# A lora-up on 128 rows, its decay map on ScalarE, and chunk ends stored by ScalarE's queue

## The chip, the cores and the metric

The kernel runs on one core of a Trainium2 chip. A core has five engines with a queue of instructions each, which run side by side and wait for each other by semaphores: TensorE (PE: matrix products into the accumulator memory PSUM; its weight loads are listed apart as PEld), VectorE (DVE), ScalarE (ACT), GpSimd (POOL) and SyncE (SP), which here only issues memory transfers (DMAs). ScalarE and GpSimd can issue DMAs too. The metric is the device time of one execution in microseconds (us), the median over runs.

## What is computed

One layer of a diffusion backbone over 128 context and 2048 latent tokens of width 1024, in float32. The part that the change touches is the preparation of the operands of a bidirectional RWKV-7 scan, for two directions e, from low-rank ("lora") projections:

```python
lw = jnp.tanh(jnp.einsum('btd,edl->betl', hf, lp['decay_down']))
w = lp['decay_w0'][None, :, None, :] + jnp.einsum('betl,elc->betc', lw, lp['decay_up'])
decay = jnp.exp(-jnp.exp(-jax.nn.softplus(-w) - 0.5))
la = jnp.einsum('btd,edl->betl', hf, lp['iclr_down'])
a = jax.nn.sigmoid(lp['iclr_bias'][None, :, None, :] + jnp.einsum('betl,elc->betc', la, lp['iclr_up']))
kk = _heads(kf * lp['kk_scale'])
kk = kk * lax.rsqrt(jnp.maximum(jnp.sum(kk * kk, axis=-1, keepdims=True), 1e-24))
kd = kf[:, None] * (1.0 + (a - 1.0) * lp['ka_scale'])
```

`decay_up` and `iclr_up` are 64 x 512 for each direction. The log of the decay is -0.6065 sigmoid(w) (DEC is exp(-0.5)), and the kernel takes sigmoid(w) as (tanh(w/2) + 1) / 2. It sums it along time inside chunks of 64 tokens; exponentials of that sum scale the scan's operands.

## The kernel before

Three phases follow each other: `phase1` (projections, lora, short convolution; to about 920 us), `phase2` (the scan in 17 stages) and `phase3` (output projection). Phase 1 goes three times (`THIRD`) over two blocks of tokens, five blocks of 384 and the last of 256. In each pass group A (the scan's operands) runs over four groups g of 128 channels and the two blocks j; so there are 24 calls of `groupA`, "blocks" below. Group B (the convolution) follows.

All products are float32 split into a high part (float32r) and a rest. A dense product (lines 157 to 159) is 24 products of 128 x 128 weights on a block's columns. In `groupA` TensorE makes, by their accumulators' names: k (mmk), r (mmr), eight lora-up products (up), the head sum of k squared (pss, line 201 on the high part hsh and line 202 on the rest hsl), v (mmv), the gate g (mmg), a second head sum for the bonus (psb, the same two lines), and three transposes of v (psv, line 403).

`lup` makes a lora-up in two products. `lora_down` has laid x out on 128 partitions so that, for direction d, rows 64d to 64d + 63 hold the high part and the other 64 the rest. The first (line 355) multiplies by the weights' high part, which lies on both halves; the second (line 356) by the weights' rest, on the 64 rows with the high part of x alone. `load_up` splits the weights: the rests of both directions share one tile, one on each half.

Then, for each direction: tanh on ScalarE (361), the affine map on VectorE (362), the sum along time on VectorE (365 or 367), two exps on ScalarE (370 into pp, with a column for the shift; 371 in place), products on VectorE into four rotating buffers sp, each stored by SyncE's queue (`spill`). Line 382 stores the last column of each chunk of pp, 128 x 6 values, by SyncE's queue too. `part_sum` splits what it sums: the high part by ScalarE (193), the rest by GpSimd (194) into hsl, one buffer for all. `shifted` copies the accumulator into a padded row buffer (rawl, three of them) and sums neighbours on GpSimd (313: shk, shr, shv). Transposed v goes without its mean to vt (413, one buffer), stored by line 414. `gate_rows` makes the output gate beside group B.

The order on each engine is not that of the source. A scheduler in the build places every instruction by a model of time, so an edit moves instructions far from it as well; each engine then runs its queue strictly in that order.

Of the kernel before, what the change touches and what calls it, by code (L numbers as in the profile page):

```python
# [18 lines left out]
DEC = 0.6065306597126334  # L19
# [30 lines left out]
def phase1(K):  # L50
    nc, tc, A, S = K.nc, K.tc, K.A, K.S
    V, G, P, T = nc.vector, nc.gpsimd, nc.scalar, nc.tensor
    cp = Pool(K, "p1c", "left")
    wp = Pool(K, "p1w", "left", 2)
    hl = Pool(K, "p1h", "left", 2)
    tp = Pool(K, "p1t", "left")
    ca = Pool(K, "p1ca", "right")
    hr = Pool(K, "p1hr", "right")
    ta_ = Pool(K, "p1ta", "right")
# [5 lines left out]
    make_identity(nc, idt)  # L65
    vec = cp.tile([128, NV], F32, name="vec")
    nc.sync.dma_start(vec[:], A["vec"])
    ones = ta_.tile([128, 128], F32, tag="upraw", name="ones", bufs=1)
    nc.sync.dma_start(ones[:], A["cst"][:, 0:128])
    onr = cp.tile([128, 128], F32R, name="onr")  # L70
    V.tensor_copy(onr[:], ones[:])
# [4 lines left out]
    V.memset(eps[:], 1e-6)  # L76
    nln2 = cp.tile([128, 1], F32, name="nln2")
    V.memset(nln2[:], -0.6931471805599453)
    dv = cp.tile([128, ND], F32, name="dv")

    def ts(o, i, s1, s2=None, o0=ALU.mult, o1=ALU.add, eng=V):
# [20 lines left out]
    def load_up():  # L102

        raw = ta_.tile([128, 2, 2, 512], F32, tag="x", name="upraw", bufs=1)
        for h in range(2):
            nc.sync.dma_start(raw[h * 64:h * 64 + 64], A["wup"].rearrange("n (d p) c -> p n d c", d=2))
        parts = ca.tile([128, 6, 512], F32R, tag="upx", name="ups")
        hi, lo = parts[:, 0:4].rearrange("p (n d) c -> p n d c", d=2), parts[:, 4:6]
        for n in range(2):
            V.tensor_copy(hi[:, n], raw[:, n])  # L110
            for d in range(2):
                r = slice(d * 64, d * 64 + 64)
                V.tensor_tensor(lo[r, n], raw[r, n, d], hi[r, n, d].bitcast(F32), ALU.subtract)
                up[n, d] = (hi[:, n, d], lo[:, n])

    kept = set()

# [71 lines left out]
    def parts_of(t_, n, nm, eng):  # L189

        hi = ta_.tile([128, 384], F32R, tag="hsh", name=f"hsh{nm}", bufs=1)
        lo = ta_.tile([128, 384], F32R, tag="hsl", name=f"hsl{nm}", bufs=1)
        P.copy(hi[:, :n], t_[:, :n])  # L193
        eng.tensor_tensor(lo[:, :n], t_[:, :n], hi[:, :n].bitcast(F32), ALU.subtract)  # L194
        return hi, lo
# [25 lines left out]
    hsl = [hr.tile([128, 8, 512], F32, tag="h", name="wadas0")]  # L221
# [14 lines left out]
    for i, b in enumerate((0, 2, 1, 3)):  # L236
        pr = pmm.tile([128, 512], F32, tag="mm", name=f"psrow{b}")
        for k2 in range(2):
            wt = hsl[i][:, k2 * 4:k2 * 4 + 4] if i < 3 else hsl[k2 + 1][:, 8:12]
            nc.sync.dma_start(wt, A["wada"][b][:, k2 * 4:k2 * 4 + 4])  # L240
            mod_rows(pr, wt, range(k2 * 4, k2 * 4 + 4))
        if i == 0:
            x0 = load_x(0)
        if i == 1:
            wlora = [load_w(32), load_w(33)]
            x1 = load_x(1, ca, "upx")
        if i == 2:
            ws0 = [load_w(cb) for cb in (4, 0)]
        rows = ta_.tile([128, 512], F32, tag="upraw", name=f"modrow{b}", bufs=1)
        V.tensor_copy(rows[:], pr[:])  # L250
        hf = b % 2
        if hf not in psm:
            psm[hf] = pax.tile([128, 8, 2], F32, tag="ax", name=f"psmod{hf}")
        for cb in range(4):
            T.matmul(psm[hf][:, b // 2 * 4 + cb, :], rows[:, cb * 128:(cb + 1) * 128], sel[:], start=True, stop=True)
        if b >= 2:

            gs = cp.tile([128, 4, 2], F32, name=f"gs{hf}")
            sh = cp.tile([128, 4, 2], F32, name=f"sh{hf}")
            ad = lambda v: vec[:, v + hf * 4:v + hf * 4 + 4].unsqueeze(2).broadcast_to((128, 4, 2))  # L260
            V.tensor_tensor(sh[:], psm[hf][:, 0:4, :], ad(V_BSH), ALU.add)
# [12 lines left out]
    first_products(wlora + ws0, range(4, 8))  # L274


    NRAW = 3
    rawl = [cp.tile([128, 6, 66], F32, name=f"rawl{i}") for i in range(NRAW)]
    rawc = [cp.tile([128, 130], F32, name=f"rawc{i}") for i in range(1)]
    for t_ in rawl:  # L280
# [46 lines left out]
    def groupA(g, j, ws, hh, lw, pre):  # L327
        t0, n = BLK[j]
# [16 lines left out]
        rS = shifted(psr or dense(wr_, hh, n, "r"), j, 0, g, "r", 1)  # L345
        kds = []
        for d in range(2):
            rows = slice(d * 64, d * 64 + 64)
            cs = slice(g * 128, g * 128 + 128)

            def lup(which):
                ps = pmm.tile([128, 384], F32, tag="mm", name=f"up{which}_{K.u()}")
                hi, lo = up[which, d]
                x = lw[which * 2 + d]
                T.matmul(ps[:, :n], hi[:, cs], x[:, :n], start=True, stop=False)
                T.matmul(ps[:, :n], lo[rows, cs], x[rows, :n], start=False, stop=True)
                return ps

            psw = lup(0)
            t = tl("t", 2)  # L360
            P.activation(t[:, :n], psw[:, :n], AF.Tanh, bias=dcol(D_W0H + d * 4 + g), scale=0.5)
            V.tensor_scalar(t[:, :n], t[:, :n], -0.5 * DEC, -0.5 * DEC, ALU.mult, ALU.add)
            c = t
            if d == 0:
                V.tensor_tensor_scan(c[:, :n], smask[:, :n], t[:, :n], 0.0, ALU.mult, ALU.add)
            else:
                V.tensor_tensor_scan(c[:, :n][:, ::-1], smask[:, :n], t[:, :n][:, ::-1], 0.0, ALU.mult, ALU.add)
            pt = rot(pp[d], "pp")
            c3 = c[:, :n].rearrange("p (a b) -> p a b", b=64)
            P.activation(pt[:, :nch, 1 - d:65 - d], c3, AF.Exp)  # L370
            P.activation(c[:, :n], c[:, :n], AF.Exp, bias=nln2[:], scale=-1.0)
            psa = lup(1)
            ta = tl("ta", 2)
            P.activation(ta[:, :n], psa[:, :n], AF.Tanh, bias=dcol(D_IBH + d * 4 + g), scale=0.5)
            v3 = lambda x_: x_[:, :n].rearrange("p (a b) -> p a b", b=64)
            al = tl("sp", 4)
            V.tensor_tensor(v3(al), v3(kk), pt[:, :nch, d:64 + d], ALU.mult)
            spill(f"al{d}", g, j, al, "al")
            rh = tl("sp", 4)
            V.tensor_tensor(v3(rh), v3(rS), pt[:, :nch, 1 - d:65 - d], ALU.mult)  # L380
            spill(f"rh{d}", g, j, rh, "rh")
            nc.sync.dma_start(S[f"pc{d}"][g * 128:(g + 1) * 128, t0 // 64:t0 // 64 + nch], pt[:, :nch, 64 - 64 * d])
# [8 lines left out]
            V.scalar_tensor_tensor(be[:, :n], ta[:, :n], 1.0, kkn[:, :n], ALU.add, ALU.mult)  # L391
# [113 lines left out]
    def gate_rows():  # L505
        for b in range(2):
            pr = pmm.tile([128, 512], F32, tag="mm", name=f"psgr{b}")
            for k2 in range(4):
                wt = wp.tile([128, 2, 512], F32, tag="wr", name=f"wgate{b}{k2}", bufs=2)
                nc.sync.dma_start(wt[:], A["wada"][4 + b][:, k2 * 2:k2 * 2 + 2])  # L510
                mod_rows(pr, wt, (k2 * 2, k2 * 2 + 1))
                yield
            rows = ta_.tile([128, 512], F32, tag="upraw", name=f"gaterow{b}", bufs=1)
            P.copy(rows[:], pr[:])
            pg = pmm.tile([2, 512], F32, tag="mm", name=f"psgate{b}")
            T.matmul(pg[:], sel[:], rows[:], start=True, stop=True)
            gr = ta_.tile([2, 512], F32, tag="upraw", name=f"gate{b}", bufs=1)
            nc.sync.dma_start(gr[:], A["bgate"][:, b * 512:(b + 1) * 512].broadcast_to((2, 512)))
            V.tensor_tensor(gr[:], pg[:], gr[:], ALU.add)
            nc.sync.dma_start(S["gate"][:, b * 512:(b + 1) * 512], gr[:])  # L520


    up = {}
# [818 lines left out]
```

## Time and profile before

| | us |
|---|---|
| runs of before | 1814.86, 1816.56, 1825.39; median 1816.56 |
| the profiled execution | 1812.69 |
| its span, first to last instruction | 1810.9 |
| mean granted TensorE clock | 0.968 of full speed |
| group A, first, middle and last pass | 69 to 245, 407 to 602, 744 to 900 |

Engines' busy time counts neither waiting nor the issue of DMAs. TensorE's products overlap in the records: each lasts about twice the distance to the next start, so its speed is read from starts. A timeline row has start, duration, engine, source line, operation, tiles out<-in, rows*columns of the weights where it is a product, shapes, and in brackets the idle time before it and what ended it. DMA rows show the issue; the time from issue to landing stands apart.

### The profile page before, as it was taken

How to read it: one execution, taken by the hardware profiler on the slowest of the kernel's cores; microseconds unless marked ns; L12 is line 12 of the kernel's file. 1: busy time of each engine (PE TensorE's matmuls, PEld its weight loads, DVE VectorE, ACT ScalarE, POOL GpSimd, SP SyncE). 2: the span in 40 equal slices, each digit the busy share in tenths (PEclk: the TensorE clock that was granted, in tenths of full speed). 3: DMA queues.
4: the chain of work that ended last, by engine and by line, in shares of the span. 5: the costliest groups of instructions: out<-in, count | busy, mean ns of one | idle time of the engine just before them, and what ended most of it. 6: DMA issues, size and time to landing. Idle time of an engine off the chain costs nothing. (4 is left out here: it accounts for less than half of the span.)

```text
span 1810.9 us, 35097 instructions
## 1 busy us (share of the span) xinstructions
PE 1695.7 (94%) x13424; PEld 1534.4 (85%) x13424; DVE 1227.7 (68%) x2281; ACT 818.9 (45%) x1559; POOL 593.7 (33%) x1091
## 2 busy tenths in 40 slices
PE   5999999999999999999999899998998999898998
PEld 2988889999888999989999888888888888676886
DVE  5889987547877445588833457687777888858443
ACT  4555544214444122254431366666566666542222
POOL 0122210002222000122218247767676777322221
PEclk7899999999999999999999999999999999898999
DMA  9778886655666634487767466567668765645442
GB/s 355 215 231 236 236 244 241 234 212 143 186 180 185 187 121 144 135 234 233 202 229 263 107 146 160 145 178 164 156 167 177 178 159 131 169 154 186 144 147 93
DMA packets 315528, 335.36 MB, mean 185 GB/s; under 512 B 166936, under 2 KB 263704, under 8 KB 301280
## 3 DMA queue, kind: packets, MB, share of 16 engines
q1 hardware_dynamic: 278640, 324.20, 61.1%
q10 hardware_dynamic: 35360, 4.46, 1.6%
q0 software_dynamic: 1360, 4.46, 0.7%
q8 instruction: 106, 1.74, 0.4%
q14 instruction: 62, 0.51, 0.1%
HBM read 221.22 MB, written 111.82 MB: 184 GB/s over the span
## 5 line engine op out<-in xcount | busy, mean ns | idle before, releaser
L877 POOL TENSOR_TENSOR zt<-zt,ztmp 128x30 f32<-128x30 f32 (+7 forms) x510 | 205.6, 403 | 39.2
L949 PE MATMUL psE<-str,stl 128*128 128x128 f32 x1088 | 154.7, 288 | 12.5 <-DVE E L950 10.9
L949 PEld LDWEIGHTS psE<-str,stl 128*128 128x128 f32 x1088 | 136.0, 197 | 19.3 <-DVE E L950 12.1
L874 POOL TENSOR_TENSOR ztmp<-ab,zt 128x60 f32<-128x60 f32 (+7 forms) x255 | 135.3, 531 | 19.4
L722 ACT COPY bd<-rr 64x512 f32<-64x512 f32 x136 | 83.9, 617 | 79.4 <-PE psF L835 24.7
L950 DVE TENSOR_TENSOR E<-psE,msk 128x512 f32<-128x512 f32 x136 | 93.4, 689 | 26.4 <-PE psE L949 23.9
L313 POOL TENSOR_TENSOR shk<-rawl 128x384 f32<-128x384 f32 (+1 forms) x24 | 21.8, 908 | 251.7 <-ACT rawl L309 248.2
L996 PE MATMUL psS<-sv,E 128*64 128x64 f32 x1056 | 94.2, 237 | 8.2 <-DVE sv L1008 7.0
L962 PE MATMUL psY<-E,sv 128*64 128x64 f32 x1088 | 98.3, 233 | 2.2 <-DVE E L950 2.2
L996 PEld LDWEIGHTS psS<-sv,E 128*64 128x64 f32 x1056 | 68.4, 139 | 34.3 <-DVE sv L1008 11.2
L1008 DVE TENSOR_TENSOR sv<-psS,pc 64x128 f32<-64x128 f32 x254 | 72.4, 285 | 30.7 <-PE psS L996 22.7
L1278 POOL TENSOR_TENSOR z<-z,x 128x512 f32<-128x512 f32 x32 | 42.8, 1340 | 137.8 <-DVE z L1274 102.7
L835 PE MATMUL psG<-rr,bd 128*128 128x128 f32 x544 | 79.6, 287 | 7.2 <-DVE F L836 5.6
L835 PE MATMUL psF<-rr,bd 128*128 128x128 f32 x544 | 79.0, 287 | 7.1 <-issue 5.0
L938 PE MATMUL psX<-F,zb 128*128 128x128 f32 x544 | 73.3, 284 | 10.1 <-DVE E L950 5.8
L835 PEld LDWEIGHTS psG<-rr,bd 128*128 128x128 f32 x544 | 68.9, 195 | 10.6 <-DVE F L836 5.9
L938 PEld LDWEIGHTS psX<-F,zb 128*128 128x128 f32 x544 | 65.9, 195 | 13.8 <-DVE E L950 6.8
L962 PEld LDWEIGHTS psY<-E,sv 128*64 128x64 f32 x1088 | 71.9, 139 | 6.7 <-issue 3.7
L835 PEld LDWEIGHTS psF<-rr,bd 128*128 128x128 f32 x544 | 68.6, 196 | 10.2 <-issue 6.6
L157 PE MATMUL mmv<-h,w 128*128 128x384 f32 (+1 forms) x192 | 68.0, 354 | 4.4 <-ACT q1r L311 4.4
L194 POOL TENSOR_TENSOR hslb<-kd,hshb 128x384 fp32r<-128x384 f32 (+1 forms) x24 | 25.2, 1050 | 134.5 <-ACT hshb L193 133.0
L157 PE MATMUL mmg<-h,w 128*128 128x384 f32 (+1 forms) x192 | 63.6, 331 | 4.3 <-ACT rawc L316 2.3
(315 smaller groups left out, 5380.0 us busy)
## 6 DMA issues: line engine op xcount, KB each, us to landing
w<-scr_wsp SPq DMA_DIRECT2D x68, 1024.0 KB, 6.9
scr_wsp<-w SPq DMA_DIRECT2D x34, 1024.0 KB, 6.4
rr<-scr_ops SPq DMA_DIRECT2D x64, 512.0 KB, 4.8
scr_ops<-sp SPq DMA_DIRECT2D x160, 192.0 KB, 4.9
wr<-in_win SPq DMA_DIRECT2D x34, 512.0 KB, 6.9
ab<-scr_at SPq DMA_DIRECT2D x34, 256.0 KB, 4.1
x<-in_x SPq DMA_DIRECT2D x17, 512.0 KB, 4.0
wadas<-in_wada SPq DMA_DIRECT2D x8, 1024.0 KB, 13.1
```

The lines of the kernel that those rows point to most:

```text
L157: T.matmul(ps[:, :n], w[:, 0, k], hh[:, 0, k, :n], start=k == 0, stop=False)
L722: (V.tensor_copy if k in ON_DVE else P.copy)(dst, src)
L835: T.matmul(ps[:, i, :].rearrange("p (a b) -> p a b", b=64), w[:, u, :], x[:, :, u, :], start=True, stop=True)
L874: G.tensor_tensor(tv, ab[:, j:j + 2, j + 2:32].unsqueeze(1).broadcast_to((128, kn, 2, n)), zt[:, :kn, j:j + 2].unsqueeze(3).broadcast_to(( ...
L877: G.tensor_tensor(zt[:, :kn, j + 2:32], zt[:, :kn, j + 2:32], tv[:, :, r], ALU.subtract)
L938: T.matmul(px[:, i, :], B.zb[:, gi, us.start + i, :], g.F[:, us.start + i, :], start=True, stop=True)
L949: T.matmul(pe[:, i, hd, :].rearrange("p (b t) -> p b t", b=2), g.lt[:, :, hd, us.start + k + i].rearrange("p b t -> p (b t)"), g.rt[:, :, ...
L950: V.tensor_tensor(g.E[n][:, k:k + 2].rearrange("p a b c -> p (a b) c"), pe[:].rearrange("p a b c -> p (a b) c"), B.msk[:, ME[g.d]].unsquee ...
L962: T.matmul(ys[gi][hd * 64:(hd + 1) * 64, u, :], v[:, hd, :], e[:, hd, 64:128], start=True, stop=True)
L996: T.matmul(sp[r, hd, :], g.E[n][:, k, hd, 0:64], sv[:, u, hd, :], start=True, stop=True)
L1008: V.tensor_tensor(dst, sp[r], B.pc[r, 2 * p:2 * p + 2, c:c + 1].broadcast_to((64, 2, 64)), ALU.mult)
L1278: (V if last else G).tensor_tensor(z[:, cs], z[:, cs], xt[:, cs], ALU.add)
```

## The change

Four things are edited. `load_up` makes the weights' rest on 128 rows for both directions, and `lup` multiplies it with all of x. The affine map on VectorE becomes an activation that adds 1 on ScalarE, and its factor moves into the scales of the two exps. The chunk ends are stored by ScalarE's queue. And four kilobytes a partition are found for the longer tile: hsl shares vt's buffer, there are two padded row buffers instead of three, and rows of 512 (ones, modrow, gaterow, gate) share the buffer of group B's pv.

```diff
@@ phase1
-    ones = ta_.tile([128, 128], F32, tag="upraw", name="ones", bufs=1)
+    ones = tp.tile([128, 128], F32, tag="pv", name="ones", bufs=1)
...
+    one1 = cp.tile([128, 1], F32, name="one1")
+    V.memset(one1[:], 1.0)
@@ load_up
-        parts = ca.tile([128, 6, 512], F32R, tag="upx", name="ups")
-        hi, lo = parts[:, 0:4].rearrange("p (n d) c -> p n d c", d=2), parts[:, 4:6]
+        parts = ca.tile([128, 8, 512], F32R, tag="upx", name="ups")
+        hi, lo = [parts[:, i:i + 4].rearrange("p (n d) c -> p n d c", d=2) for i in (0, 4)]
         for n in range(2):
             V.tensor_copy(hi[:, n], raw[:, n])
+            V.tensor_tensor(lo[:, n], raw[:, n], hi[:, n].bitcast(F32), ALU.subtract)
             for d in range(2):
-                r = slice(d * 64, d * 64 + 64)
-                V.tensor_tensor(lo[r, n], raw[r, n, d], hi[r, n, d].bitcast(F32), ALU.subtract)
-                up[n, d] = (hi[:, n, d], lo[:, n])
+                up[n, d] = (hi[:, n, d], lo[:, n, d])
@@ parts_of
-        lo = ta_.tile([128, 384], F32R, tag="hsl", name=f"hsl{nm}", bufs=1)
+        lo = ta_.tile([128, 384], F32R, tag="vt", name=f"hsl{nm}", bufs=1)
@@ phase1
-    NRAW = 3
+    NRAW = 2
@@ groupA
-                T.matmul(ps[:, :n], lo[rows, cs], x[rows, :n], start=False, stop=True)
+                T.matmul(ps[:, :n], lo[:, cs], x[:, :n], start=False, stop=True)
...
-            V.tensor_scalar(t[:, :n], t[:, :n], -0.5 * DEC, -0.5 * DEC, ALU.mult, ALU.add)
+            P.activation(t[:, :n], t[:, :n], AF.Identity, bias=one1[:])
...
-            P.activation(pt[:, :nch, 1 - d:65 - d], c3, AF.Exp)
-            P.activation(c[:, :n], c[:, :n], AF.Exp, bias=nln2[:], scale=-1.0)
+            P.activation(pt[:, :nch, 1 - d:65 - d], c3, AF.Exp, scale=-0.5 * DEC)
+            P.activation(c[:, :n], c[:, :n], AF.Exp, bias=nln2[:], scale=0.5 * DEC)
...
-            nc.sync.dma_start(S[f"pc{d}"][...], pt[:, :nch, 64 - 64 * d])
+            nc.scalar.dma_start(S[f"pc{d}"][...], pt[:, :nch, 64 - 64 * d])
@@ gate_rows (and modrow likewise)
-            rows = ta_.tile([128, 512], F32, tag="upraw", name=f"gaterow{b}", bufs=1)
+            rows = tp.tile([128, 512], F32, tag="pv", name=f"gaterow{b}", bufs=1)
...
-            gr = ta_.tile([2, 512], F32, tag="upraw", name=f"gate{b}", bufs=1)
+            gr = tp.tile([2, 512], F32, tag="pv", name=f"gate{b}", bufs=1)
```

GpSimd's queue in the middle pass, before, over two blocks: sh is a neighbour sum, hsls and hslb are the rests for the head sums pss and psb; the first number behind hsls or hslb is the block j, the last ones only tell buffers apart, and the brackets list the engines and DMA queues waited for.

```order
L313 TENSOR_TENSOR shk_4301<-rawl_465 128x384 [waits Activation_49,Pool_49]
L194 TENSOR_TENSOR hsls_2_4308<-sq_2_505_4305,hshs_2_4307 128x384 [waits PE_49,Activation_49]
L313 TENSOR_TENSOR shr_4347<-rawl_466 128x384 [waits Activation_49]
L313 TENSOR_TENSOR shv_4450<-rawl_464 128x384 [waits DVE_49,Activation_49]
L194 TENSOR_TENSOR hslb_2_4416<-kd_2_517_4372,hshb_2_4415 128x384 [waits PE_49,Activation_49]
L313 TENSOR_TENSOR shk_4524<-rawl_465 128x384 [waits Activation_49,Pool_49]
L194 TENSOR_TENSOR hsls_3_4531<-sq_3_540_4528,hshs_3_4530 128x384 [waits PE_49,Activation_49]
L313 TENSOR_TENSOR shr_4570<-rawl_466 128x384 [waits Activation_49]
L313 TENSOR_TENSOR shv_4673<-rawl_464 128x384 [waits DVE_49,Activation_49]
L194 TENSOR_TENSOR hslb_3_4639<-kd_3_552_4595,hshb_3_4638 128x384 [waits PE_49,Activation_49]
```

The same place after (line numbers are one higher there):

```order
L314 TENSOR_TENSOR shr_4344<-rawl_467 128x384 [waits Activation_49]
L195 TENSOR_TENSOR hsls_2_4305<-sq_2_505_4302,hshs_2_4304 128x384 [waits DMAHW7_49,DVE_49,Activation_49]
L314 TENSOR_TENSOR shv_4447<-rawl_466 128x384 [waits Activation_49]
L195 TENSOR_TENSOR hslb_2_4413<-kd_2_517_4369,hshb_2_4412 128x384 [waits PE_49,Activation_49]
L314 TENSOR_TENSOR shk_4521<-rawl_467 128x384 [waits Activation_49]
L314 TENSOR_TENSOR shr_4567<-rawl_466 128x384 [waits DVE_49,Activation_49]
L195 TENSOR_TENSOR hsls_3_4528<-sq_3_540_4525,hshs_3_4527 128x384 [waits DMAHW4_49,DVE_49]
L314 TENSOR_TENSOR shv_4670<-rawl_467 128x384 [waits DVE_49,Activation_49]
L314 TENSOR_TENSOR shk_4752<-rawl_466 128x384 [waits DVE_49,Activation_49]
L195 TENSOR_TENSOR hslb_3_4636<-kd_3_552_4592,hshb_3_4635 128x384 [waits PE_49,Activation_49]
```

The hsls of a block now waits for a DMA (DMAHW), the store of vt, where it waited for TensorE and ScalarE; and it stands behind shr, where it stood ahead of it.

ScalarE's queue, before, behind the lora-ups of one block of the middle pass:

```order
L361 ACTIVATE t_3_547_4577<-up_546_4574,dv 128x384
L374 ACTIVATE ta_3_549_4586<-up_548_4583,dv 128x384
L361 ACTIVATE t_3_556_4608<-up_555_4605,dv 128x384
L374 ACTIVATE ta_3_558_4617<-up_557_4614,dv 128x384
L385 ACTIVATE kd_3_552_4595<-ta_3_549_4586,dv,vec 128x384
L385 ACTIVATE kd_3_561_4626<-ta_3_558_4617,dv,vec 128x384
L370 ACTIVATE pp_0_476<-t_3_547_4577 128x6x64
L371 ACTIVATE t_3_547_4577<-t_3_547_4577,nln_112 128x384
L309 COPY rawl_464<-mmv_4645 128x6x64
L311 ACTIVATE q1v_4671<-mmv_4645,dv 128x384
L370 ACTIVATE pp_0_477<-t_3_556_4608 128x6x64
```

And after:

```order
L361 ACTIVATE t_3_556_4605<-up_555_4602,dv 128x384
L374 ACTIVATE ta_3_558_4614<-up_557_4611,dv 128x384
L362 ACTIVATE t_3_547_4574<-t_3_547_4574,one_114 128x384
L385 ACTIVATE kd_3_552_4592<-ta_3_549_4583,dv,vec 128x384
L362 ACTIVATE t_3_556_4605<-t_3_556_4605,one_114 128x384
L385 ACTIVATE kd_3_561_4623<-ta_3_558_4614,dv,vec 128x384
L370 ACTIVATE pp_0_475<-t_3_547_4574 128x6x64
L370 ACTIVATE pp_0_476<-t_3_556_4605 128x6x64
L310 COPY rawl_467<-mmv_4642 128x6x64
L312 ACTIVATE q1v_4668<-mmv_4642,dv 128x384
L371 ACTIVATE t_3_547_4574<-t_3_547_4574,nln_112 128x384
L382 DMA scr_pc_58<-pp_0_475 128x6x1
```

The two activations of line 362 have come in behind the tanhs, and the two stores of line 382 behind the exps.

More of the change, by code (lines that the diff above doesn't have):

```diff
@@ L248, in phase1 @@
             ws0 = [load_w(cb) for cb in (4, 0)]
-        rows = ta_.tile([128, 512], F32, tag="upraw", name=f"modrow{b}", bufs=1)
+        rows = tp.tile([128, 512], F32, tag="pv", name=f"modrow{b}", bufs=1)
         V.tensor_copy(rows[:], pr[:])
@@ L347, in groupA @@
         for d in range(2):
-            rows = slice(d * 64, d * 64 + 64)
             cs = slice(g * 128, g * 128 + 128)
@@ L381, in groupA @@
             spill(f"rh{d}", g, j, rh, "rh")
-            nc.sync.dma_start(S[f"pc{d}"][g * 128:(g + 1) * 128, t0 // 64:t0 // 64 + nch], pt[:, :nch, 64 - 64 * d])
+            nc.scalar.dma_start(S[f"pc{d}"][g * 128:(g + 1) * 128, t0 // 64:t0 // 64 + nch], pt[:, :nch, 64 - 64 * d])
             kd = tl("kd", 2)
```

## The prediction

> **What bounds the kernel now.** I read the profile in this order: the stretches of the span with each engine's busy time, then TensorE's timeline in one block, then who waits for whom, then the DMA issues. Stretches first. The four rows are the three group-A passes (the first, middle and last third of the tokens) and everything from the scan on; the columns are the window, its length, busy us of PE, PEld, DVE, ACT and POOL with counts, the granted clock, and the DMA share.
>
> ```profile
> span 1810.9 us, 35097 instructions
> ...
> core 0: us, PE busy (x) PEld busy (x) DVE busy (x) ACT busy (x) POOL busy (x), PEclk, DMA share, GB/s
> ...
> 69.00:245.00 176.00, 168.76 (x882) 153.77 (x881) 159.50 (x247) 99.61 (x194) 36.99 (x37) 0.99 0.82 244
> ...
> 407.00:602.00 195.00, 183.75 (x936) 168.60 (x936) 144.83 (x231) 86.69 (x171) 40.20 (x40) 0.96 0.65 178
> ...
> 744.00:900.00 156.00, 153.74 (x954) 142.72 (x953) 123.86 (x230) 76.83 (x170) 36.43 (x41) 1.00 0.73 208
> ...
> 920.00:1811.00 891.00, 821.26 (x8590) 726.10 (x8589) 577.96 (x1106) 441.48 (x821) 469.68 (x942) 0.96 0.60 161
> ```
>
> TensorE is busy 94 to 99% of all three group-A passes, so what it stops doing there shortens them, unless something else is close behind. In the first pass something is: VectorE has 159.5 of 176 us. In the other two it has 74 and 79%. ScalarE never passes 57%, so it has room for work. The change touches only these 527 us.
>
> But busy is not the same as producing. The timeline of TensorE alone shows the end of a dense product (lines 158 and 159), then one block's eight lora-up products, whose second halves (line 356) contract 64 rows:
>
> ```profile
> start us, us, engine line op out<-in xcount [idle before <-releaser]
> ...
> 456.47 0.33 PE L158 MATMUL mmr<-h,w 128*128 128x384 f32 x1
> 456.64 0.34 PE L159 MATMUL mmr<-h,w 128*128 128x384 f32 x1
> 456.82 0.33 PE L355 MATMUL up<-lw,ups 128*128 128x384 f32 x1
> 457.08 0.43 PE L356 MATMUL up<-lw,ups 64*128 64x384 f32 x1
> 457.44 0.44 PE L355 MATMUL up<-lw,ups 128*128 128x384 f32 x1
> 457.82 0.43 PE L356 MATMUL up<-lw,ups 64*128 64x384 f32 x1
> 458.18 0.44 PE L355 MATMUL up<-lw,ups 128*128 128x384 f32 x1
> 458.56 0.44 PE L356 MATMUL up<-lw,ups 64*128 64x384 f32 x1
> 458.92 0.45 PE L355 MATMUL up<-lw,ups 128*128 128x384 f32 x1
> 459.30 0.44 PE L356 MATMUL up<-lw,ups 64*128 64x384 f32 x1
> 462.41 0.69 PE L201 MATMUL pss<-hshs,onr 128*128 128x384 f32 x1 [2.67 <-ACT hshs L193]
> ```
>
> Read the first column, not the durations. Dense products start 0.175 us apart ((456.82 - 456.47) / 2). So does the first lora-up product after a dense one: 0.18, because both use 128 rows. Then the starts spread to 0.37 ((459.30 - 457.08) / 6). Each crossing between a 128-row and a 64-row product costs 0.195 us, in both directions; the very first costs 0.26 - 0.175 = 0.085. The same view of another block, with the weight loads, says what is lost:
>
> ```profile
> 435.44 0.19 PEld L159 LDWEIGHTS mmr<-h,w 128*128 128x128 f32 x1
> 435.62 0.34 PE L159 MATMUL mmr<-h,w 128*128 128x384 f32 x1
> ...
> 436.24 0.18 PEld L356 LDWEIGHTS up<-lw,ups 64*128 64x128 f32 x1 [0.25 <-issue]
> 436.24 0.44 PE L356 MATMUL up<-lw,ups 64*128 64x384 f32 x1
> ```
>
> A 128-row product has its weights loaded 0.18 us ahead, under the product before it. A 64-row product that follows a 128-row one starts its load only at its own recorded start. The 0.18 us of the load comes out from under cover.
>
> **The change part by part.** *Both halves on 128 rows.* The counts and medians of the two lines:
>
> ```profile
> L355 PE MATMUL up<-lw,ups x96: 279/439/446, 69.4 to 881.3; 128*128 128x384 f32 x80, 128*128 128x256 f32 x16
> L356 PE MATMUL up<-lw,ups x96: 379/436/684, 69.7 to 881.7; 64*128 64x384 f32 x80, 64*128 64x256 f32 x16
> ```
>
> Ninety-six pairs are 24 blocks of eight products. Eight now take 459.30 - 456.82 = 2.48 plus one more interval of 0.37, so 2.85 us; at 0.175 they would take 1.40. That is 1.45 us a block, 34.8 us in all, 11.6 in each pass. For the 16 pairs of 256 columns I take the same excess, since it is that of a load. The arithmetic of the product itself gets no cheaper: the interval goes by columns, not rows.
>
> The Trainium skill, TensorEngine Tiling (Array Packing), section Tiling Modes, says that changing the tiling mode drains TensorE, which agrees with the extra interval. But TensorE: Matmul & The Clock Gate, in its drain step, puts a drain at about 128 cycles of 2.4 GHz, by my estimate 0.053 us; 192 crossings would then be worth only 10 us and not 35. The measured 0.195 is nearly four times that, so the row decides.
>
> Not all of the 11.6 arrives in the first pass: VectorE's 159.5 lose 16 instructions of 0.35 us (next part), 5.6, and its 16.5 us of idle time are partly TensorE's own pace. If all of them stayed, the pass would end at 170.4; if TensorE sets it, at 164.4. I take the middle, which gives back 3 us; both ends (0 and 6) go to the range.
>
> *The affine map.* VectorE loses 48 of line 362; ScalarE gains 48 activations with a bias, priced by line 342, the nearest in form:
>
> ```profile
> L362 DVE TENSOR_SCALAR t<-t x48: 281/352/1116, 73.6 to 889.5; 128x384 f32<-128x384 f32 x40, 128x256 f32<-128x256 f32 x8
> ...
> L342 ACT ACTIVATE kk<-ok,vec x24: 494/604/647, 65.8 to 881.7; 128x384 f32<-128x384 f32 x20, 128x256 f32<-128x256 f32 x4
> ...
> L842 ACTq DMA_DIRECT2D scr_at<-dg x34: 366/366/436, 924.8 to 1521.0; - x34
> ...
> L382 SPq DMA_DIRECT2D scr_pc<-pp x48: 370/371/1118, 76.4 to 891.6; - x48
> ...
> DMA to landing us min/median/max: 3.9/7.3/11.1
> ```
>
> VectorE saves 16.9 us and ScalarE takes 29.0. On the chain tanh, map, scan, exp it adds 0.25 us less one change of engine. ScalarE goes from 99.6 to about 109 us in the first pass: cover enough, so zero, with 0 to +3 for products queued behind it. The scales in the two exps cost nothing, they ride in instructions that exist.
>
> *Chunk ends by ScalarE's queue.* Two issues of about 0.37 us a block move from SyncE to ScalarE (the 0.366 is what its queue takes for another store). ScalarE waits there only for its own exp, and the order puts another exp between; behind it stand the copies that free TensorE's accumulators. 48 x 0.366 = 17.6 us over 24 blocks, on an engine with 40% to spare: zero. SyncE's queue loses 48 waits for ScalarE, so the stores behind them can start earlier; VectorE's waits for those stores, shown next, could shrink. I take zero, and 6 us of gain as the far end.
>
> ```profile
> DVE sp L377 <- DMA scr_ops<-sp: 15.2, 3, 7.5
> DVE sp L391 <- DMA scr_ops<-sp: 14.6, 8, 4.6
> ```
>
> (waits of VectorE in the middle pass: total, times, longest). The results wait for a free buffer, that is for an earlier store to land; TensorE's 2.67 us at 462.41 is what reaches it of such waits.
>
> *Room for the longer weight tile: the new wait.* The low part of each head sum (hsl, line 192) now lives in the buffer of vt. GpSimd may write hsls of a block only after the block before has its vt stored and landed; before, it waited for ScalarE's rounding alone. Behind it in GpSimd's queue stands the neighbour sum of v. TensorE's second head-sum product (line 202) reads hsls, so all that follows it on TensorE waits too, and VectorE's clamp (line 339), which reads the sum. How tight it is:
>
> ```profile
> 435.12 0.49 PE L403 MATMUL psv<-idt,ov 128*128 128x128 f32 x3
> 436.99 0.56 DVE L413 SCALAR_TENSOR_TENSOR vt<-vmean,psv 128x384 f32<-128x384 f32 x1
> 437.58 0.37 SPq L414 DMA_DIRECT2D scr_vt<-vt  x1
> 438.13 1.41 POOL L194 TENSOR_TENSOR hsls<-sq,hshs 128x384 fp32r<-128x384 f32 x1 [4.22 <-ACT hshs L193]
> ...
> 504.32 0.49 PE L403 MATMUL psv<-idt,ov 128*128 128x128 f32 x3
> 509.56 0.37 SPq L414 DMA_DIRECT2D scr_vt<-vt  x1
> 509.64 1.00 POOL L194 TENSOR_TENSOR hsls<-sq,hshs 128x384 fp32r<-128x384 f32 x1 [3.64 <-ACT hshs L193]
> ...
> L414 SPq DMA_DIRECT2D scr_vt<-vt x24: 370/371/1556, 97.0 to 903.9; - x24
> ...
> DMA to landing us min/median/max: 1.9/3.6/10.7
> ```
>
> From transpose (psv) to store takes 2.5 us in one kind of block and 5.2 in the other; landing adds 3.6 (median); GpSimd 1.0. So hsls is ready 7.1 or 9.8 us after the transposes. In the new order some 85 to 100 products of TensorE lie between the transposes and the next block's second head-sum product in the first pass, 15 us and more: no wait. In the last two passes it alternates: about eight blocks have 44 to 50 products between, 7.7 to 8.8 us at 0.175, the other eight 70 to 96, 12 us and more. The eight tight ones are met within -1.7 and +2.1 us. I take 1 us for each, 8 us, as nearer to the upper row since a late start has company: after the 2.67 us of idleness at 462.41 the product takes 0.69 us instead of 0.34, and the middle pass, with 11 us idle, lost another 8 to a clock of 0.96 (0.04 x 195), 0.7 us for each us idle. Ends: 0, and 2.1 in all eight with that loss, 2.1 x 8 x 1.7 = 29.
>
> The third padded row buffer goes as well. Its reader, a neighbour sum on GpSimd, is two dense products (8 us) ahead of the copy that would wait; zero. The 512-column rows at the start and for the gate share a buffer with pv of group B, at times when no pv is alive; zero. Splitting the weights is two operations of 1024 columns on 128 rows for four of 512 on 64; zero.
>
> *From the scan on* nothing is edited, but the scheduler orders it afresh, since its model of the first half changed. No row prices that. 70 of the 891 us have TensorE idle; I take 0, and 8 us to either side.
>
> **Sum.** -34.8 + 3 + 8 = -23.8 us. The profiled execution took 1812.69 us, 1.8 more than its span; it would be 1788.9. The median of the runs is 1816.56, 0.2% above the profiled one; from it, 1792.8, so I say 1793.
>
> **The rivals.**
>
> *One: all of it arrives.* The store lands in time, and earlier issues shorten VectorE's waits: -34.8 - 6 gives 1776. For it: the median landing; TensorE's 94 to 99%. Against: the first pass, where VectorE is at 91%.
>
> *Two: the new wait eats the gain.* At the far end, 29 us, with 3 for VectorE, the time is 1816.6 - 34.8 + 3 + 29 = 1814, no change. For it: the slower kind of block above, and the drop of the clock behind a stall. Against it: the new order puts the slower kind where there is more room.
>
> *Three: slower, by the same wait.* It decides above (34.8 - 3) / 1.7 = 19 us of TensorE waiting, 2.3 us in each tight block. If half of the 16 stores land like the longest row, 10.7, hsls comes 7 us later there, 5 beyond what the order leaves on average: 8 x 5 x 1.7 = 68 us, and 1816.6 - 31.8 + 68 = 1853. For it: the same queue carries the 1 MB weight loads. Against: 3.6 is the median, so half land sooner.
>
> *Four: the products don't speed up.* If a load could run ahead only when the rows used differ from those of the product in flight, 128-row pairs would stay at 0.37, nothing is gained, and the new wait's 8 us give 1825. Against it stand the starts at 456.64 and 456.82, and the load at 435.44. The Trainium skill, TensorE: Matmul & The Clock Gate, section on packing small matmuls, states such a rule (a load overlaps only with a different row group); the load at 435.44 overlaps without one, so here the trace differs.
>
> **How the numbers follow.** Forecast 0.61 (its own range 1782 to 1804, by 3 us either side from VectorE and 8 from the part behind the scan), rival one 0.16, two 0.13, three 0.07, four 0.03. What a measurement of this kernel can tell from no change is about 1%, 18 us: below 1798.4, or above 1834.7. Of the forecast, three quarters lie below 1798.4 (0.46), with rival one 0.62 faster; the rest of the forecast, two and four make 0.31 the same; three is 0.07 slower. The range reaches from 1775, the first rival, to 1819, past the second, and leaves out some 0.2.
>
> **What would show it.** Right: starts of lines 355 and 356 0.175 apart, weight loads of line 356 ahead of their product; VectorE without line 362, ScalarE with 48 more activations. The new wait: idle time of GpSimd before hsls put down to the vt store, and of TensorE before the second pss product. Wrong: starts still at 0.37; the middle pass no shorter than 195 us; or a change of more than 8 us behind the scan.

## The result and the profile after

The changed kernel took 1794.59 us (median of 4 runs, 1792.30 to 1797.57), the kernel before 1815.71 beside it: a ratio of 0.9875, 95% interval 0.9834 to 0.9916. The forecast was 1793. Of all the runs told of below, one was in a slower state of the chip (a run of rows_sp6r1, 2270.05 us at a mean granted clock of 0.656), and the ratios leave it out. The profiled execution took 1792.30 us, at a mean granted clock of 0.979 (before 0.968). Its page:

```profile
span 1790.5 us, 35059 instructions
...
PE 1665.3 (93%) x13424; PEld 1529.4 (85%) x13424; DVE 1215.8 (68%) x2232; ACT 836.8 (47%) x1607; POOL 601.1 (34%) x1089
```

To compare, both traces are cut at the same events. Group A of a pass goes from its first lora product (a lora-up, line 355, in the first pass, a product of the projection into the lora, mml, in the other two) to the first product of group B; the scan goes to the first product of the output phase. Cut so, the passes of before start and end up to 17 us from the rounded windows used so far. Columns as in the prediction's first view. Before:

```profile
69.40:237.20 167.80, 160.56 (x836) 145.57 (x835) 151.61 (x236) 93.80 (x183) 35.92 (x36) 0.99 0.82 239
389.90:588.70 198.80, 191.52 (x981) 176.81 (x981) 146.45 (x235) 86.26 (x170) 39.19 (x39) 0.96 0.60 168
730.20:887.90 157.70, 155.44 (x976) 144.56 (x975) 119.53 (x227) 74.56 (x165) 33.94 (x39) 1.00 0.68 194
1030.20:1616.30 586.10, 534.75 (x7072) 477.69 (x7071) 429.52 (x846) 364.69 (x648) 375.05 (x803) 0.96 0.66 160
```

After:

```profile
69.20:235.00 165.80, 150.27 (x836) 146.00 (x835) 148.77 (x223) 101.52 (x199) 44.07 (x36) 0.98 0.85 247
388.40:582.80 194.40, 177.25 (x980) 172.52 (x980) 138.11 (x217) 91.15 (x186) 39.30 (x39) 0.97 0.71 175
719.80:876.40 156.60, 148.65 (x976) 145.34 (x974) 113.18 (x209) 80.43 (x178) 33.77 (x38) 0.98 0.69 193
1019.00:1596.70 577.70, 538.43 (x7072) 478.30 (x7071) 435.69 (x847) 362.64 (x648) 375.21 (x803) 0.98 0.65 162
```

Read length and PE together. In the three passes TensorE is busy 507.5 us before and 476.2 after, 31.3 less. Yet the passes shrank from 524.3 to 516.8, by 7.5 us: TensorE's idle time in them (length less busy time) rose from 16.8 to 40.6. The scan, where nothing was edited, shrank by 8.4 us, the start and group B by 3.8, the output phase by 0.7. The time came out as forecast, but from other places.

The products did what was meant. TensorE's timeline with the weight loads, in one block:

```profile
454.08 0.19 PEld L355 LDWEIGHTS up<-lw,ups 128*128 128x128 f32 x1
454.25 0.34 PE L355 MATMUL up<-lw,ups 128*128 128x384 f32 x1
454.25 0.19 PEld L356 LDWEIGHTS up<-lw,ups 128*128 128x128 f32 x1
454.43 0.34 PE L356 MATMUL up<-lw,ups 128*128 128x384 f32 x1
454.60 0.34 PE L355 MATMUL up<-lw,ups 128*128 128x384 f32 x1
454.78 0.33 PE L356 MATMUL up<-lw,ups 128*128 128x384 f32 x1
```

Starts are 0.175 us apart, and each load runs ahead under the product before. Of the 23.8 us of new idle time the largest part, 14.9, stands before v's first product (busy, mean ns, idle time before it by releaser); 8.2 more stand before the head sums. Before:

```profile
L157 PE MATMUL mmv<-h,w 128*128 128x384 f32 (+1 forms) x192 | 68.0, 354 | 4.4 <-ACT q1r L311 4.4
```

After:

```profile
L158 PE MATMUL mmv<-h,w 128*128 128x384 f32 (+1 forms) x192 | 68.5, 357 | 19.3 <-ACT q1r L312 11.3 <-ACT rawc L317 8.1
```

TensorE now stands 19.3 us before v, waiting for ScalarE. The timeline of the three engines in the block shown above:

```profile
458.91 0.33 PE L356 MATMUL up<-lw,ups 128*128 128x384 f32 x1
...
459.04 0.56 DVE L388 TENSOR_TENSOR sp<-kd,t 128x384 f32<-128x384 f32 x1 [1.68 <-DMA scr_ops<-sp]
459.51 0.61 DVE L320 SCALAR_TENSOR_TENSOR ok<-shk,dv,q1k 128x384 f32<-128x384 f32 x1
...
460.16 0.62 ACT L343 ACTIVATE kk<-ok,vec 128x384 f32<-128x384 f32 x1 [2.67 <-DVE ok L320]
...
461.19 0.46 ACT L310 COPY rawl<-mmr 128x384 f32<-128x384 f32 x1
461.55 0.58 ACT L312 ACTIVATE q1r<-mmr,dv 128x384 f32<-128x384 f32 x1
...
462.18 0.44 PE L158 MATMUL mmv<-h,w 128*128 128x384 f32 x1 [2.94 <-ACT q1r L312]
```

Read it from the last row back. Dense products and lora-ups share five accumulators (mm). At this point r holds one and the four lora-ups the other four, so v needs the one that q1r empties. ScalarE's queue runs in order: the two reads of r stand behind kk, kk waits for VectorE's ok, and ok stands behind a result that waits for a store of sp. Eight lora-up products took 2.85 us before and take 1.40 now, so TensorE comes to such a wait up to 1.45 us earlier. That is not the whole of it: no_rows, below, keeps the 64-row products and waits in this block too.

### The profile page after: what moved, and what is told of

The parts are those of the page before. It is cut to its first block, busy times and chain, and to the rows that moved or that the text cites. A ratio compares the mean times of both kernels' runs of the same rounds, so it can differ in the third digit from the quotient of the medians.

```text
span 1790.5 us, 35059 instructions
## 1 busy us (share of the span) xinstructions
PE 1665.3 (93%) x13424; PEld 1529.4 (85%) x13424; DVE 1215.8 (68%) x2232; ACT 836.8 (47%) x1607; POOL 601.1 (34%) x1089
## 5 line engine op out<-in xcount | busy, mean ns | idle before, releaser
L877 POOL TENSOR_TENSOR zt<-zt,ztmp 128x30 f32<-128x30 f32 (+7 forms) x510 | 201.8, 396 | 39.3
L996 PE MATMUL psS<-sv,E 128*64 128x64 f32 x1056 | 102.3, 235 | 7.3 <-DVE sv L1008 7.2
L962 PE MATMUL psY<-E,sv 128*64 128x64 f32 x1088 | 107.2, 234 | 0.1
L996 PEld LDWEIGHTS psS<-sv,E 128*64 128x64 f32 x1056 | 73.2, 138 | 35.3 <-DVE sv L1008 9.1
L158 PE MATMUL mmv<-h,w 128*128 128x384 f32 (+1 forms) x192 | 68.5, 357 | 19.3 <-ACT q1r L312 11.3
L962 PEld LDWEIGHTS psY<-E,sv 128*64 128x64 f32 x1088 | 76.9, 139 | 4.6 <-issue 2.1
L195 POOL TENSOR_TENSOR hsls<-sq,hshs 128x384 fp32r<-128x384 f32 (+1 forms) x24 | 30.4, 1265 | 110.9 <-ACT hshs L194 29.1
```

Of the source, the lines that this page charges most:

```text
L158: T.matmul(ps[:, :n], w[:, 0, k], hh[:, 0, k, :n], start=k == 0, stop=False)
L877: G.tensor_tensor(zt[:, :kn, j + 2:32], zt[:, :kn, j + 2:32], tv[:, :, r], ALU.subtract)
L962: T.matmul(ys[gi][hd * 64:(hd + 1) * 64, u, :], v[:, hd, :], e[:, hd, 64:128], start=True, stop=True)
L996: T.matmul(sp[r, hd, :], g.E[n][:, k, hd, 0:64], sv[:, u, hd, :], start=True, stop=True)
```

## The experiments

Each kernel is the changed one with the edit shown, unless said otherwise. Lengths of group A (three passes together) and of the scan, in us, with TensorE's idle time in group A:

| kernel | median | group A | idle in A | scan |
|---|---|---|---|---|
| before | 1815.71 | 524.3 | 16.8 | 586.1 |
| before, profiled again | 1824.54 | 530.7 | 20.7 | 589.3 |
| after | 1794.59 | 516.8 | 40.6 | 577.7 |
| rows_only | 1790.26 | 515.3 | 38.4 | 570.5 |
| no_rows | 1804.38 | 527.7 | 17.6 | 578.5 |
| hsl_own | 1812.16 | 531.7 | 48.5 | 569.9 |
| sp5 | 1789.08 | 510.4 | 34.4 | 573.5 |
| pc_sp | 1803.23 | 516.2 | 35.9 | 591.9 |
| bufs_only | 1807.61 | 528.9 | 21.0 | 576.7 |
| rows_sp5 | 1773.12 | 500.7 | 29.3 | 578.0 |
| norows_sp5 | 1781.26 | 510.5 | 9.1 | 579.4 |
| affdve_sp5 | 1771.74 | 506.1 | 30.1 | 570.8 |
| rows_sp6r1 | 1760.80 | 489.4 | 21.0 | 578.0 |
| mm6 | 1773.93 | 489.4 | 21.7 | 577.5 |

Lengths come from one profile each, and a median stands beside its own runs of before, whose medians were 1815.71 to 1820.68. The second profile of before, unchanged, says how far they can be trusted:

> The kernel before, unchanged, for a second profile: how far the lengths of the stretches repeat. Expected: group A 524 us within 4, the scan 586 us within 4. If they scatter more, differences of 8 us between single profiles mean little.

Group A came out 6.4 us longer, the scan 3.2. Against this profile the changed kernel's group A is 13.9 us shorter, not 7.5, so what arrived there is known no better than that. Smaller differences of one pair are not read below. Nor is the profiled execution always near the median: of rows_only and hsl_own it was the fastest run (1782.96 and 1801.87 us), of no_rows and pc_sp the slowest.

An edit can also give TensorE another order in group A. Of the pairs below, after and no_rows have the same order there, product for product, and so have rows_sp5 and norows_sp5; bufs_only and rows_only have it in the last two passes. In the other comparisons of group A the order moved with the edit.

**The long products alone (rows_only).** Map and chunk ends go back to VectorE and SyncE:

```diff
-            P.activation(t[:, :n], t[:, :n], AF.Identity, bias=one1[:])
+            V.tensor_scalar(t[:, :n], t[:, :n], -0.5 * DEC, -0.5 * DEC, ALU.mult, ALU.add)
...
-            nc.scalar.dma_start(S[f"pc{d}"][...], pt[:, :nch, 64 - 64 * d])
+            nc.sync.dma_start(S[f"pc{d}"][...], pt[:, :nch, 64 - 64 * d])
```

> Kept of the change: the 128-row lora-up and the shared buffers. Undone: the affine map is back on VectorE, the chunk ends are back on SyncE's queue. Theory 1 (TensorE's saving of 34.8 us is real, and what gave most of it back in group A is VectorE waiting for the stores of sp): TensorE's interval stays 0.175 us, VectorE has 17 us more to do and its stores wait behind the chunk ends again, so it is 2 to 10 us slower than the changed kernel, 1797 to 1805. Theory 2 (ScalarE's extra 29 us of activations and 17.6 us of issues, in the queue that frees TensorE's accumulators, gave it back): faster than the changed kernel by 8 us or more, under 1787.

1790.26 us, 0.9838 of before (0.9787 to 0.9889), which lies between the expectations. Group A is as after; map and stores are worth nothing there that one profile can tell. TensorE's idle time is as long, but stands elsewhere, in another order: 19.8 us of it before the first head sum (pss), 5.5 before v.

**All but the long products (no_rows).** The rest's product goes back to its 64 rows:

```diff
+            rows = slice(d * 64, d * 64 + 64)
...
-                T.matmul(ps[:, :n], lo[:, cs], x[:, :n], start=False, stop=True)
+                T.matmul(ps[:, :n], lo[rows, cs], x[rows, :n], start=False, stop=True)
```

> Undone of the change: the second lora-up product contracts 64 rows again. All else as in the changed kernel. Both theories: the starts in a run of eight spread to 0.37 us again. Theory 1: TensorE's waits in the three group-A passes (40.7 us in the changed kernel, 16.8 before) shrink as its own work grows, back under 25 us, and the time is within 8 us of before, 1807 to 1820. Theory 2: the time is above that of before by 10 us or more, since ScalarE's part is then a pure loss.

1804.38 us, 0.9903 (0.9867 to 0.9940), some 3 us under the first theory's range. Group A is 10.9 us longer than after and TensorE's idle time back at 17.6. The order is the same, so this is what the rows do: they are worth 10.9 us of the passes, a third of the 34.8, and 23.0 us of TensorE's saving come back as idle time. About 7 of these stand before v (12.5 us here, 19.3 in after), about 12.5 before the head sums. And v in the block shown above:

```profile
464.66 0.69 PE L158 MATMUL mmv<-h,w 128*128 128x384 f32 x1 [3.57 <-ACT q1r L312]
```

3.57 us here, 2.94 in after. (Behind this wait the products start 0.32 us apart until 468.98, and 0.175 after that, so part of what a wait costs shows as busy time.) So the slow lora-ups don't cover this wait. Of the 19.3 us before v, 12.5 come with the rest of the change (its buffers, its work on ScalarE or its order), where before had 4.4. TensorE's order in the scan is the same in after, rows_only and no_rows, and its scan stays short, so that gain is not the rows'.

**Without the new wait (hsl_own).** hsl gets its own buffer back:

```diff
-        lo = ta_.tile([128, 384], F32R, tag="vt", name=f"hsl{nm}", bufs=1)
+        lo = ta_.tile([128, 384], F32R, tag="hsl", name=f"hsl{nm}", bufs=1)
```

> The changed kernel with a buffer for hsl of its own, so that no head sum waits for the store of vt. Theory 1: GpSimd's 17.8 us of waiting for that store in the middle pass go, but TensorE hardly waited for them (its waits for hsls are 1.5 and 0.5 us in first and last pass), so the time changes by less than 5 us, 1790 to 1799. Theory 3 (the new wait is what gave the saving back): TensorE's waits in group A fall by 10 us or more, 1785 or less.

1812.16 us, 0.9969 (0.9943 to 0.9996): slower than after, which none of the theories had. The scheduler, free of the wait, laid the blocks out anew: in the middle pass the bonus sum (psb) now stands 17 to 18 products of r behind k. TensorE's wait for psb's rounded operand in that pass:

```profile
PE psb L202 <- ACT hshb L194: 14.1, 7, 3.4
```

(total, times, longest); VectorE's waits for stores there grew from 23.8 to 40.6 us. So the run does not price the wait; the order moved with it. In the changed kernel itself the waits are these; GpSimd's in the middle pass:

```profile
POOL hsls L195 <- DMA scr_vt<-vt: 17.8, 7, 3.4
```

and TensorE's in the whole run:

```profile
PE pss L203 <- POOL hsls L195: 2.4, 3, 1.5
```

GpSimd waits 17.8 us for the store of vt, and 2.4 us of waiting for hsls reach TensorE. What reaches it by way of the neighbour sums behind hsls in GpSimd's queue isn't parted from its other waits.

**The shared buffers alone (bufs_only).** Before, with the edits of `parts_of`, NRAW and the rows of 512:

```diff
-        lo = ta_.tile([128, 384], F32R, tag="hsl", name=f"hsl{nm}", bufs=1)
+        lo = ta_.tile([128, 384], F32R, tag="vt", name=f"hsl{nm}", bufs=1)
...
-    NRAW = 3
+    NRAW = 2
```

> The kernel before with the shared buffers alone: hsl in vt's buffer, two padded row buffers, rows of 512 in pv's. No lora-up, no affine map, no queue changed. If sharing costs nothing in group A (theory 1), its three passes stay within 5 us of the 524.3 of before, and the time within 1% of before; if the new wait costs what was forecast (8 us) or more, the passes take 532 or more. The scan has a third order here: 570 to 586 us.

1807.61 us, 0.9948 (0.9924 to 0.9971). Group A lies between the two profiles of before, so no cost of the sharing shows in its length; the scan has an order of its own, and is 9.4 us shorter. The new wait itself is there. GpSimd's and TensorE's, over all of phase 1:

```profile
POOL hsls L194 <- DMA scr_vt<-vt: 54.0, 11, 9.9
PE pss L202 <- POOL hsls L194: 9.5, 6, 4.7
```

Before, TensorE never waited for hsls. Against rows_only, which adds the rows to this kernel, group A is 13.6 us longer: a third pair that prices the rows.

**Chunk ends back to SyncE's queue (pc_sp).** Line 382 alone, as in rows_only.

> The changed kernel with the chunk ends back on SyncE's queue. The scheduler then gives TensorE in the scan exactly the order of the kernel before. If the 8.4 us that the scan became shorter by the change come from its order alone, the scan takes 586 us again (within 4), where the changed kernel had 577.7; if they come from elsewhere, it stays at 574 to 581. Group A: if the waits of SyncE's queue for ScalarE's exp matter, the three passes together are more than 5 us longer than the changed kernel's 516.9; if ScalarE's issues cost more, shorter.

1803.23 us, 0.9908 (0.9873 to 0.9942). Group A is as long as after's, in another order; the scan changes:

```profile
1024.10:1616.00 591.90, 538.88 (x7072) 482.15 (x7071) 429.05 (x847) 364.31 (x648) 373.90 (x803) 0.95 0.66 158
```

It is as long as before's, and TensorE's order in it is before's, instruction for instruction. (The profiled execution was the slowest of six, 1811.92, so the scan of the median is some us shorter.) The eleven profiles with the four other orders have 569.9 to 579.4 us, the three with this one 586.1 to 591.9. Nothing in the scan is edited, so its gain goes with the order that the scheduler happened to give it. One order alone scatters as much (six kernels with the scan of hsl_own: 569.9 to 579.4), so the size of the gain is known only roughly. The granted clock goes along: 0.95 to 0.96 in the three long scans, 0.97 to 0.98 in the others. Whether it is part of the cause or follows from the order, and what in the order is better, was not followed up.

**More room for results (sp5).** Five buffers sp instead of four, at lines 376, 379, 387, 390 and 422:

```diff
-            al = tl("sp", 4)
+            al = tl("sp", 5)
```

> The changed kernel with five buffers for the stored products (sp) instead of four. Theory 1: VectorE's waits for those stores (31 us in the middle pass, 8 in the first, 16 in the last) shrink by a third or more, TensorE's waits in group A fall from 40.7 to about 28 us, and the time by 8 to 15 us, to 1780 to 1787. Theories 2 and 3: less than 5 us of change.

1789.08 us, 0.9823 (0.9784 to 0.9861), two above the expectation. VectorE's waits for stores in the middle pass fall from 23.8 to 13.3 us, and group A by 6.4, which is as much as two profiles of before differ by. The wait before v is 4.4 us here with five accumulators and the fast products; most of the idle time stands before the head sums.

**Five sp with the rows alone (rows_sp5), and the same without the rows (norows_sp5).** rows_only with `tl("sp", 5)`; then with the edit of no_rows as well.

> The 128-row lora-up and the shared buffers, the affine map on VectorE, the chunk ends on SyncE's queue, and five buffers sp. If the two gains add (rows alone 1790, five buffers 5 us), 1780 to 1788; group A under 510 us. If VectorE is then the bound by its own work, no better than rows alone: 1788 to 1794.

> As the run with the 128-row lora-up, five buffers sp, the map on VectorE and the chunk ends on SyncE's queue (1773 us, group A 500.8 us), but the second lora-up product contracts 64 rows again. TensorE's order in the scan is the same in both, so the difference lies before it. With four buffers the 128 rows were worth 11 to 14 us of group A. Theory 1 (the buffers sp held the rest of the 34.8 us back): with five they are worth 22 us or more: group A 523 or more, 1794 to 1806 us. If something else holds it back: 11 to 15 us again, group A 512 to 516, 1782 to 1789.

1773.12 us, 0.9740 (0.9706 to 0.9775), below both expectations, and 1781.26, 0.9801 (0.9776 to 0.9825). If the stores of sp were what swallowed the gain, the rows had to be worth 22 us or more of group A here. The sums over the three passes, without the rows:

```profile
sum 510.50, PE 501.39 PEld 462.21 DVE 419.90 ACT 254.72 POOL 117.90; mean PE 167.13 PEld 154.07 DVE 139.97 ACT 84.91 POOL 39.30
```

and with them:

```profile
sum 500.70, PE 471.43 PEld 459.67 DVE 418.34 ACT 250.04 POOL 115.94; mean PE 157.14 PEld 153.22 DVE 139.45 ACT 83.35 POOL 38.65
```

TensorE does 30.0 us less, the passes shrink by 9.8, in the same order. That theory fell: a fifth sp helps both versions, and the rows are worth the same third. The idle time before v is 3.7 us without the rows and 15.3 with them.

**The map on VectorE with chunk ends on ScalarE (affdve_sp5).** sp5 with the map as in rows_only.

> The changed kernel with five buffers sp and the affine map back on VectorE; the chunk ends stay on ScalarE's queue. Same order of TensorE in the scan as with five buffers otherwise. With the map on ScalarE and five buffers group A took 510.4 us; with map and chunk ends both moved back 500.8. If the map on ScalarE costs this, 499 to 504 and 1771 to 1778; if ScalarE's issues cost it, 507 to 513 and 1783 to 1791.

1771.74 us, 0.9742 (0.9713 to 0.9770). Group A, 506.1, lies between the two expectations and within the scatter of both neighbours, and against sp5 2.7 us of the lower time are the scan's. What the map costs on ScalarE stays open, within that scatter of 6 us.

**Six accumulators (mm6).** The changed kernel with one accumulator moved from the pool of sums and transposes:

```diff
-    pmm = Pool(K, "pmm", "left", 5, PSUM)
-    pax = Pool(K, "pax", "right", 3, PSUM)
+    pmm = Pool(K, "pmm", "left", 6, PSUM)
+    pax = Pool(K, "pax", "right", 2, PSUM)
```

> The changed kernel with six accumulators for products (mm) instead of five, and two instead of three for the head sums, transposes and norms. In group A the accumulators of r and of four lora-ups are all five, so v's product cannot start before ScalarE has emptied one; TensorE idles 19.4 us before it in the changed kernel, 4.4 in the one before, whose slow lora-ups left ScalarE 1.45 us more. Theory 4 (this is the largest part of what was given back): idle time before v falls under 8 us, and group A from 516.9 by 6 us or more, to 511 or less. If the accumulators only pass the lateness of VectorE and ScalarE on, the idle time moves to other products, mostly the head sums, and group A stays within 5 us of 516.9, or grows, as two accumulators for the sums are too few.

1773.93 us, 0.9775 (0.9742 to 0.9807), 21 us below after. Stretches as above:

```profile
69.90:224.50 154.60, 146.33 (x829) 142.84 (x828) 139.10 (x212) 97.86 (x193) 39.14 (x35) 1.00 0.87 253
382.10:564.40 182.30, 174.69 (x980) 170.69 (x980) 137.25 (x216) 91.39 (x187) 38.62 (x39) 0.99 0.75 188
699.90:852.40 152.50, 146.64 (x976) 143.82 (x976) 111.95 (x209) 78.26 (x176) 33.55 (x38) 0.99 0.71 201
997.40:1574.90 577.50, 532.61 (x7071) 475.50 (x7070) 435.44 (x847) 362.74 (x648) 373.35 (x803) 0.98 0.65 162
```

and v's first product:

```profile
L158 PE MATMUL mmv<-h,w 128*128 128x384 f32 (+1 forms) x192 | 63.2, 329 | 0.4 <-ACT t L361 0.4
```

The wait before v is gone, 19.3 to 0.4 us. Group A falls by 27.4, to 34.9 below before: 18.9 us of it are idle time, 8.5 busy time of TensorE. The scan stays, and the start and group B take some 6 us back. That v waited for a free accumulator is shown by this. That the accumulators are worth the 27.4 is not: the scheduler laid group A out anew, as in hsl_own. In the first block of the middle pass, for one, 11 products of v now stand between the lora-ups and the head sum that came right behind them. And the 64-row products with six accumulators were not run, so how much of the 27.4 they would have gained too is open. 17.5 us of idle time now stand before pss.

**Six sp, one padded row (rows_sp6r1).** rows_only with `tl("sp", 6)` and `NRAW = 1`.

> As the run of 1773 us, with a sixth buffer sp, for which the second padded row buffer goes. If waiting for stores still costs, another 3 to 8 us go, 1765 to 1770. If one row buffer makes ScalarE's copies, which free TensorE's accumulators, wait for GpSimd's neighbour sums, it is slower: above 1776.

1760.80 us, 0.9679 (0.9645 to 0.9713), some 4 us under the expectation: the fastest kernel of the study. Group A is 489.4, as with mm6, with five accumulators: 4.5 us are left before v, where rows_sp5 had 15.3. The reading is that with more room VectorE is late less often and ScalarE's copies come sooner; the run does not part sp from the padded row. It also says that a sixth accumulator isn't needed for a group A of 489.4. Six sp and six accumulators together were not run.

## Why the prediction came out

The time was right, 1794.59 for 1793, by luck: two errors nearly cancelled. Group A gave up 16.3 us less than the sum had, and the scan, the start, group B and the output phase, all at zero in the sum, became 12.9 us shorter.

**What failed: "TensorE is busy 94 to 99% of all three group-A passes, so what it stops doing there shortens them".** The saving was there (31.3 us of TensorE's busy time for the 34.8 forecast), but the passes gave up 7.5 us where the sum had 23.8. In the two pairs with the same order the rows take 34.0 and 30.0 us off TensorE's busy time and 10.9 and 9.8 off the passes; two thirds come back as idle time. The sum had no term for what TensorE then waits for: accumulators, before v, and the operands of the head sums. The text did name the copies, "behind it stand the copies that free TensorE's accumulators", and then costed the queue at zero since ScalarE had "40% to spare". A share says nothing of when: in the block shown, ScalarE's copies stood behind a wait for VectorE. How the loss divides between the accumulators and the other engines' lateness stays open: it is 7 us before v and 12.5 before the head sums in one pair, 11.6 and 7.1 in the other, and with a sixth accumulator (mm6) or more room for results (rows_sp6r1) group A is 489.4, in other orders.

**The new wait, +8: over-sized for this order.** GpSimd does wait for the vt store, seven times in the middle pass; TensorE's waits for hsls add up to 2.4 us. 1.5 of these stand in the first pass, where the prediction saw no wait: there 49 products, not 85 to 100, lie between the transposes and the second head-sum product of the last block. The size hangs on the order: in bufs_only and rows_only TensorE waits 9.5 and 11.6 us for hsls, near the 8 of the sum.

**The first pass, +3 for VectorE: too small.** The pass fell by 2.0 where 8.6 were forecast. In the two pairs with the same order the rows are worth 0.3 us there (166.1 to 165.8) and 2.6 (165.9 to 163.3). VectorE works for 90% of the pass in the changed kernel, 148.8 of 165.8 us. In mm6 the pass takes 154.6, but eleven of VectorE's instructions no longer fall into it, and the share is again 90% (139.1 us). So what sets this pass, VectorE or the accumulators, stays open.

**From the scan on, 0, 8 to either side: the end was passed.** It fell by 8.4 and 0.7 us, over the 8 that the prediction named as a sign of being wrong, with the order of instructions (pc_sp) and not with work; no row of before could price it. Its other sign about lengths, a middle pass no shorter than before's, was not met, but that pass fell by 4.4 us only, to 194.4.

**The affine map and the stores, zero: held in group A,** within the scatter. The prices were right:

```profile
L362 ACT ACTIVATE t<-t,one x48: 502/619/647, 72.5 to 880.2; 128x384 f32<-128x384 f32 x40, 128x256 f32<-128x256 f32 x8
...
L382 ACTq DMA_DIRECT2D scr_pc<-pp x48: 366/366/625, 76.8 to 884.3; - x48
```

0.619 us for 0.604 forecast, and 0.366 an issue. Outside group A the queue of the stores did matter: with SyncE's the scan has before's order and its length. **The padded row buffer and the shared rows of 512, zero:** held within the scatter, by bufs_only, where the wait for hsls is in it too.

**Rivals.** Four (products at 0.37) fell with the starts at 0.175; so the rule weighed there, the Trainium skill's (TensorE: Matmul & The Clock Gate, section on packing small matmuls) that a load overlaps only with another row group, does not hold for these rows (the same section also lets a load run ahead into a background weight buffer). Two and three had the loss in the vt store; a loss of like size was there (23.8 us more idle time), with another cause, and TensorE waited no more than 2.4 us for hsls.

## What to carry to other kernels

Where one engine is to be made faster, ask what its slowness was covering: list the buffers that it fills ahead and who empties them, in which order of that queue; a busy share of 95% does not answer this. When a saving shows in busy time and not in the length, look for the products whose idle time grew, and see whose lateness they wait for; one more buffer there is worth a try. Where a scheduler orders the whole program, compare stretches by events, and count a change in untouched code as the order's, not as the edit's. In edited code, trust first the pairs in which the order stayed.

## What was not expected

Taking a wait away (hsl_own) made the kernel slower by 17.6 us, with another order of the blocks. The same scan work took 586.1 to 591.9 us in one order and 569.9 to 579.4 in four others, with no more busy time on TensorE (538.88 in the longest, 538.43 in after); the granted clock was 0.95 in the one and 0.98 in the other. And the crossings between 128-row and 64-row products, 0.195 us for most of the 192, are worth 30 us of TensorE's busy time, as rows_sp5 and norows_sp5 show side by side.
